# Two down projections in one stage, activations standing, with seven of sixteen tile pairs by Strassen's seven products

## The chip, the cores and the metric

The kernel runs on one core of a Trainium2 chip. The metric is device time in microseconds, the median of several runs of the whole kernel; lower is better.

## The reference

One transformer block over 256 tokens of width 2048 in float32: a modulated norm, input projections, a two-way recurrent mixer and a windowed attention, a gated merge, and a convolutional feed-forward part. The change lies in the last product of the feed-forward part:

```python
def conv_ffn(h, w_up, conv_w, conv_b, w_down):
    a, u = jnp.split(h @ w_up, 2, axis=-1)
    return (jax.nn.silu(depthwise_conv(a, conv_w, conv_b)) * u) @ w_down
...
        ffn_x = conv_ffn(modulate(x_mid, norm2_g[l], mod_x[:, 3], mod_x[:, 4]), w_up[l], conv_w[l], conv_b[l], w_down[l])
        new_x = x_mid + mod_x[:, 5][:, None, :] * ffn_x
```

The hidden width `D_FF` is 5632, so `w_down` is 5632 x 2048: 44 row tiles of 128 (called k or f) by 16 column tiles of 128 (called j).

## The kernel before

**Precision.** Every large product is split: an operand x becomes `hi`, a copy of x rounded to the fast float32 matmul type, and `lo` = x - `hi`. A product is then hi·hi + hi·lo + lo·hi, with float32 sums in PSUM. Activations are stored with hi and lo side by side (`gt[:, k, 1, :]` is hi, `gt[:, k, 0, :]` is lo, 256 tokens each).

**Weights.** They arrive as "halves" of 128 x 1024 values (512 KB), in the order in which they are used, in one array `wst`. `Stream.load` (line 107) takes one: a load on SyncE's queue into `raw` (4 buffers, L111), a copy on ScalarE into `whi` (3 buffers, L112), a subtraction on VectorE into `wlo` (3 buffers, L113). These three instructions carry a priority that is `LEAD` = 60 instructions earlier than where they are written, so they are placed ahead of the products that use them.

**Order.** The program is written out unrolled, and a planner orders each engine's instructions: among those that it takes to be ready, the one with the earliest priority goes first. Each engine then runs its list in that order; semaphores hold an instruction until its inputs and its buffer are there.

**Feed-forward stages.** The 44 hidden tiles are worked in groups of 16, 16 and 12 (`FF_GROUPS`): up 0, up 1, down 0, up 2, down 1, down 2. An up stage makes two columns of `w_up` a step by `duo` and evacuates them by `up_evac` (convolution, silu, product, split into `gt`). A down stage makes two output column tiles a step, also by `duo`, and adds each into the residual `xm` with the gate (`add`, L913: two `scalar_tensor_tensor` instructions of 128 x 256).

**`duo`.** Weights stand in the array, activations move. For each k and each of two output tiles, one 512-column matmul (weight hi against the activation's lo and hi) and one 256-column matmul (weight lo against the activation's hi). The output has output columns on partitions and tokens along the free side, as `xm` has.

**`natural`.** An earlier stage (line 451) uses the other form: activations stand, 512 columns of weights move, each product by `mm3` (three 512-column matmuls), and the output has tokens on partitions.

**Other names.** `ada` steps accumulate a modulation matrix on VectorE between other work (loads on GpSimd's queue, L378; sums, L383; transposes on TensorE, L391) and end in the gates; `gate2` is the last. PSUM has 8 banks: pool `mm` with 5, pool `ms` with 3. The SBUF slots "kT" and "va" hold the evacuation buffers `fs1` and `fs2` in the up stages; slot "v" holds `xa`, which is last read in the first columns of up 0.

Of the kernel before, what the change touches and what calls it, by code (L numbers as in the profile page):

```python
# [7 lines left out]
F32 = mybir.dt.float32  # L8
F32R = mybir.dt.float32r
U32 = mybir.dt.uint32  # L10
AF = mybir.ActivationFunctionType
ALU = mybir.AluOpType
AX = mybir.AxisListType

P = 128
T = 256
# [4 lines left out]
NFF = DFF // P  # L21
# [4 lines left out]
LEAD = 60  # L26
LAG = 60
RUSH = 120
# [4 lines left out]
CONSTS = [("ident", 128), ("ones", 128), ("ropec", 256), ("ropes", 256), ("amask", 256), ("hmask", 256),  # L33
          ("m64", T)]
FF_GROUPS = [(0, 16), (16, 16), (32, 12)]


def offsets(fields):
# [12 lines left out]
def block_kernel(ctx, tc, xct, prm, cst, ada2, wst, out):  # L51
    nc = tc.nc
    V, S, PE = nc.vector, nc.scalar, nc.tensor

    cons = ctx.enter_context(tc.tile_pool(name="cons", bufs=1))
    big = ctx.enter_context(tc.tile_pool(name="big", bufs=1))
    strm = ctx.enter_context(tc.tile_pool(name="strm", bufs=3))
    scr = ctx.enter_context(tc.tile_pool(name="scr", bufs=3))
    tiny = ctx.enter_context(tc.tile_pool(name="tiny", bufs=8))
    mm = ctx.enter_context(tc.tile_pool(name="mm", bufs=5, space=bass.MemoryType.PSUM))  # L60
    ms = ctx.enter_context(tc.tile_pool(name="ms", bufs=3, space=bass.MemoryType.PSUM))

    def bank(pool=None):
        pool = pool or mm
        return pool.tile([P, 512], F32, name="bank" + ("m" if pool is mm else "s"))

    def mmul(o, l, r, start, stop):
        return PE.matmul(o, l, r, start=start, stop=stop, skip_group_check=True)  # L68

    def mm3(o, lh, ll, rh, rl, start, stop):  # L70
        mmul(o, lh, rh, start, False)
        mmul(o, lh, rl, False, False)
        return mmul(o, ll, rh, False, stop)
# [11 lines left out]
    base = [1 << 30]  # L85
# [6 lines left out]
    def con(n):  # L92
        o, w = COFF[n]
        return cst_t[:, o:o + w]

    ident, ones = con("ident"), con("ones")
# [3 lines left out]
    class Stream:  # L100
# [26 lines left out]
        def next(self, n=1):  # L127
            if self.pos == 8:
                self.load()
            sl = slice(self.pos * P, (self.pos + n) * P)  # L130
            self.pos += n
            return self.hi[:, sl], self.lo[:, sl]

    st = Stream()

    def split(hi, lo, src):
        S.copy(hi, src)
        V.tensor_tensor(lo, src, hi.bitcast(F32), op=ALU.subtract)
# [41 lines left out]
    start = big.tile([P, 1024], F32, name="csr", tag="acc")  # L180
# [14 lines left out]
    def ada_mm(aps, u):  # L195
        n, per = len(chunks[u]), 4 // len(chunks[u])
        w = 256 * n
        for kt in range(KT):
            g, slot = 32 * (kt % 4), slots[groups[u][kt // 8 if n == 2 else 0] % 3][kt // per % 4]
            last_mm = mmul(aps[g:g + 32, 0:w], csr[:, kt, :], slot[:, kt % per * w:(kt % per + 1) * w], kt < 4, kt >= KT - 4)  # L200
        return last_mm
# [17 lines left out]
    def warm(n, after):  # L219
        with tc.issue_after(after.ins):  # L220
            for _ in range(n):
                last = mmul(ssq[:, 0:P], ident, ident, True, True)
        return last
# [35 lines left out]
    with tc.high_priority(offset=RUSH):  # L259
        for cnd in range(2):  # L260
            ts = slice(T * cnd, T * cnd + T)
# [4 lines left out]
    first = ada_mm(aps, 0)  # L266
    with tc.high_priority(offset=RUSH):
        first = warm(3, first)
# [9 lines left out]
    def unit(u):  # L278
        if len(chunks[u]) == 1:
            st.load(7)  # L280
            wv, w = [st.next(4)], [st.next() for _ in range(3)]
        else:
            st.load()
            wv = [st.next(4) for _ in range(2)]
            st.load(6)
            w = [st.next() for _ in range(6)]
        st.pos = 8
        return wv, w
# [19 lines left out]
    for u in range(len(chunks)):  # L308
        wv, w = unit(u)
# [91 lines left out]
    ada_it = ada_steps()  # L401

    def ada(n=1):
        with tc.high_priority(offset=-LAG), tc.issue_after(st.last.ins):
            for _ in range(n):
                next(ada_it, None)
# [3 lines left out]
    def tick():  # L410
        if tasks:
            tasks.pop(0)()

    def both(act, k):
        return act[:, k].rearrange("p a t -> p (a t)")
# [3 lines left out]
    def duo(acts, nk=KT):  # L419
        os = [bank() for _ in range(2)]  # L420
        for k in range(nk):
            ws = [st.next() for _ in range(2)]
            for o, w, act in zip(os, ws, acts):
                mmul(o, w[0], both(act, k), k == 0, k == nk - 1)
            for o, w, act in zip(os, ws, acts):
                mmul(o[:, T:], w[1], act[:, k, 1, :], False, k == nk - 1)
            if k % 4 == 3:
                tick()
        return os
# [160 lines left out]
    def hgrn_c(h):  # L590
        hs = slice(h * P, h * P + P)
        sp = bank(ms).rearrange("p (n d e) -> p n d e", n=2, d=2)
        for d in range(2):
            for a in range(2):
                PE.matmul(sp[:, 0, d], KN[:, d, a], vn[:, 2 + a, hs], start=(a == 0), stop=(a == 1))  # L595
            PE.matmul(sp[:, 1, d], KN[:, d, 2], vn[:, d, hs], start=True, stop=True)  # L596
        V.tensor_copy(SS[:, 0], sp[:, 0])
        for d in range(2):
            V.scalar_tensor_tensor(SS[:, 1, d], SS[:, 0, d], decb[:, d:d + 1], sp[:, 1, d], op0=ALU.mult, op1=ALU.add)

    def hgrn_d(h):
        hs = slice(h * P, h * P + P)
        ob = bank(ms)
        obs[h] = ob

        for a in range(2):
            mmul(ob[:, a * P:a * P + P], vn[:, a, hs], MS[:, a, :], a == 0, False)
        for d in range(2):
            for a in range(2):
                mmul(ob[:, a * P:a * P + P], SS[:, a ^ d, d], QI[:, d, a * P:a * P + P], False, d == 1)  # L610
        S.activation(OS[:, 0], ob[:, 0:T], AF.Square)

    def hgrn_e(h):
        if h < 0:
            return
        ob = obs.pop(h)
        PE.matmul(ob[:, T:], ones, OS[:, 0], start=True, stop=True)  # L617
        rsqrt(OS[:, 1], ob[:, T:], 1.0 / P)
        V.scalar_tensor_tensor(qo[:, 1, h, :], ob[:, 0:T], par("hng"), OS[:, 1], op0=ALU.mult, op1=ALU.mult)
# [50 lines left out]
    for h in range(H):  # L670
# [6 lines left out]
        if h == 6:  # L677
# [4 lines left out]
            kT = big.tile([P, 2, 512], F32, name="kT", tag="kT")  # L682
            va = big.tile([P, 4, 256], F32, name="va", tag="va")
            kv_evac(bs)
        for d in range(2):
            if 2 * h + d < 3:
                o = early_f[2 * h + d]
            else:
                o = bank()
# [4 lines left out]
        parts = [lambda h=h: hgrn_e(h - 1), lambda h=h: hgrn_b(h), lambda h=h: hgrn_c(h), lambda h=h: hgrn_d(h)]  # L694
        if h == 0:

            parts = [lambda: None, parts[1], lambda: None, parts[2], lambda: None, parts[3]]
# [126 lines left out]
    xm = big.tile([P, KT, T], F32, name="xm", tag="qo")  # L824
    for i in range(2):
        nc.sync.dma_start(xm[:, 8 * i:8 * i + 8, :], xct[:, 8 * i:8 * i + 8, 0:T])
    gate1, sc2, sh2, gate2 = [modv[:, i, :] for i in range(4)]
# [4 lines left out]
    g0 = hlf[:, 2 * KT * T:].rearrange("p (k a t) -> p k a t", a=2, k=KT)  # L832
# [53 lines left out]
    fs1 = big.tile([P, 4, T], F32, name="fs1", tag="kT")  # L886
    fs2 = big.tile([P, 4, T], F32, name="fs2", tag="va")
# [3 lines left out]
    def up_evac(g, gt, i, oa, ou, fold=fold):  # L891
        f = FF_GROUPS[g][0] + i
        t, s = fs1[:, f % 4, :], fs2[:, f % 4, :]
        fold(s, oa)
        S.activation(t, s, AF.Identity, bias=cb[:, f:f + 1], scale=cw[:, f, 1:2])  # L895
        V.scalar_tensor_tensor(t[:, 1:T], s[:, 0:T - 1], cw[:, f, 0:1], t[:, 1:T], op0=ALU.mult, op1=ALU.add)  # L896
        V.scalar_tensor_tensor(t[:, 0:T - 1], s[:, 1:T], cw[:, f, 2:3], t[:, 0:T - 1], op0=ALU.mult, op1=ALU.add)
        fold(s, ou)
        S.activation(t, t, AF.Silu)
        V.tensor_tensor(s, s, t, op=ALU.mult)  # L900
        split(gt[:, i, 1, :], gt[:, i, 0, :], s)
        if f >= 2:
            ada(1 + f % 2)

    def up(g, gt, i0=0):
        for i in range(i0, FF_GROUPS[g][1]):
            up_evac(g, gt, i, *duo((h2, h2)))

    def down(g, gt, last):
        f0, n = FF_GROUPS[g]  # L910
        def add(j, o):
            for i in range(2):
                V.scalar_tensor_tensor(xm[:, j, :], o[:, T * i:T * i + T], gate2[:, j:j + 1], xm[:, j, :],  # L913
                                       op0=ALU.mult, op1=ALU.add)

        for j in range(0, KT, 2):
            if last and j == KT - 2:
                for i in range(2):
                    add(j + i, single(gt, n))
                    nc.sync.dma_start(out[:, j + i:j + i + 1, :], xm[:, j + i:j + i + 1, :])  # L920
                continue
            for i, o in enumerate(duo((gt, gt), n)):
                add(j + i, o)
            j0 = {2: 0, 6: 4, 10: 8, 12: 12}.get(j)
            if last and j0 is not None:
                nc.sync.dma_start(out[:, j0:j + 2, :], xm[:, j0:j + 2, :])
# [3 lines left out]
    up(0, g0, 2)  # L930
    g1 = big.tile([P, 16, 2, T], F32R, name="g1", tag="b")
    up(1, g1)
    down(0, g0, False)
    up(2, g0)
    down(1, g1, False)
    down(2, g0, True)


# [154 lines left out]
```

## Time and profile before

| what | value |
|---|---|
| median of 3 runs | 1680.49 us (1680.35 to 1680.75) |
| profiled execution, first to last instruction (span) | 1680.0 us |
| TensorE (PE) busy | 1665.3 us (99%) |
| TensorE weight loads (PEld) busy | 1410.7 us (84%) |
| VectorE (DVE) busy | 1206.9 us (72%) |
| ScalarE (ACT) busy | 835.3 us (50%) |
| granted TensorE clock | 1.000 |

The page gives no time for the profiled execution other than its span; the median of the runs is 0.5 us above it. Busy is the time in which at least one instruction of an engine runs. PE and PEld are matmuls and weight loads, which overlap. In rows that list groups, `out<-in` names the tiles written and read, then follow the shape, the count, the busy time with the mean duration in ns, and the idle time before these instructions with what ended it. Rows of the chain or the timeline begin with the start and the length in us.

### The profile page before, as it was taken

The page shows a single profiled execution, that of the slowest core. Times are in us where ns is not written, and L with a number is a line of the kernel's source. Part 1 is how long each engine was busy: PE and PEld are TensorE (multiplying, and loading weights), DVE is VectorE, ACT ScalarE, POOL GpSimd, SP SyncE. Part 2 cuts the span into 40 slices and gives each one's busy share as a digit, 9 for nine tenths or more (in the row PEclk, how much of TensorE's full clock was granted, in tenths as well). Part 3 has the DMA queues.
Part 4 walks back from the last instruction along what each step waited for, and adds up shares of the span by engine and source line. Part 5 has one row for each costly group of instructions (what it writes and reads, how often), then busy time and mean ns, then how long its engine had stood idle before and what let it go on. Part 6 is the DMA issues. An engine that isn't in the chain of part 4 may idle for free.

```text
span 1680.0 us, 25442 instructions
## 1 busy us (share of the span) xinstructions
PE 1665.3 (99%) x9774; PEld 1410.7 (84%) x9774; DVE 1206.9 (72%) x1920; ACT 835.3 (50%) x1279; POOL 68.3 (4%) x132
## 2 busy tenths in 40 slices
PE   7999999999999999999999999999999999999999
PEld 4668888888888888888888988888888888888887
DVE  3448986666879886879879887777666656666565
ACT  4337543433646764455555655555555335554332
POOL 0000100000000000001000000000000000000000
PEclk9999999999999999999999999999999999999999
DMA  9987834534466668878866577687555555555564
GB/s 380 407 350 242 288 119 160 177 110 155 162 217 208 211 209 278 285 243 279 282 199 234 185 251 250 218 272 251 188 182 194 188 188 189 188 188 189 188 201 150
DMA packets 104154, 371.88 MB, mean 221 GB/s; under 512 B 11488, under 2 KB 13920, under 8 KB 104032
## 3 DMA queue, kind: packets, MB, share of 16 engines
q1 hardware_dynamic: 85600, 303.14, 52.8%
q0 software_dynamic: 18432, 67.12, 12.7%
q8 instruction: 76, 1.25, 0.3%
q14 instruction: 46, 0.38, 0.1%
HBM read 368.11 MB, written 2.10 MB: 220 GB/s over the span
## 4 chain that ended last, share of the span: by engine, by line
PE 93%; DMA 4%; issue 2%; DVE 1%; SPq 0%; ACT 0%; POOL 0%; DVEq 0%; POOLq 0%
PE bankm L68 87%; PE banks L68 4%; DMA ringv<-in_wst_dram 1%; DMA ringq<-in_wst_dram 1%; DMA ringkT<-in_wst_dram 1%; DVE wlo L113 1%; PE banks L391 0%; PE banks L595 0%; PE banks L764 0%; DMA araw<-in_ada_dram 0%; PE banks L587 0%; DMA xraw<-in_xct_dram 0%; PE banks L596 0%; PE banks L617 0%; PE banks L734 0%
## 5 line engine op out<-in xcount | busy, mean ns | idle before, releaser
L68 PE MATMUL bankm<-hl,whi 128*128 128x512 f32 (+1 forms) x3392 | 1050.6, 392 | 0.0
L113 DVE TENSOR_TENSOR wlo<-raw,whi 128x1024 fp32r<-128x1024 f32 (+1 forms) x498 | 606.7, 1219 | 314.1 <-ACT whi L112 312.3
L112 ACT CAST whi<-raw 128x1024 fp32r<-128x1024 f32 (+1 forms) x498 | 520.9, 1046 | 588.4 <-PE bankm L68 499.4
L68 PEld LDWEIGHTS bankm<-hl,wlo 128*128 128x128 f32 x3104 | 581.4, 188 | 133.7 <-DVE wlo L113 2.1
L68 PE MATMUL bankm<-hl,wlo 128*128 128x256 f32 (+2 forms) x3104 | 660.5, 287 | 1.2 <-DVE wlo L113 1.2
L68 PEld LDWEIGHTS bankm<-hl,whi 128*128 128x128 f32 x3392 | 533.8, 189 | 19.9 <-DVE fs L882 0.3
L68 PE MATMUL bankm<-whi,hl 128*128 128x512 f32 x512 | 164.7, 395 | 1.0 <-ACT hl L230 1.0
L383 DVE SCALAR_TENSOR_TENSOR acc<-araw,csil,acc 128x1024 f32<-128x1024 f32 x120 | 153.5, 1279 | 2.2 <-DMA araw<-in_ada_dram 1.8
L68 PEld LDWEIGHTS bankm<-whi,hl 128*128 128x128 f32 x512 | 95.7, 188 | 22.3 <-ACT hl L230 2.6
L378 POOL DMA_DIRECT2D araw<-in_ada_dram x128 | 68.1, 532 | 1093.5 <-DVE acc L383 579.2
L68 PE MATMUL bankm<-wlo,hl 128*128 128x512 f32 x256 | 99.6, 392 | 0.0
L68 PE MATMUL bankm<-yb,whi 128*128 128x512 f32 x256 | 80.8, 397 | 0.0
L68 PE MATMUL bankm<-g,whi 128*128 128x512 f32 x256 | 80.4, 395 | 0.0
L68 PEld LDWEIGHTS bankm<-g,wlo 128*128 128x128 f32 x256 | 48.1, 188 | 11.4
L68 PEld LDWEIGHTS bankm<-yb,wlo 128*128 128x128 f32 x256 | 48.1, 188 | 11.3
L68 PEld LDWEIGHTS bankm<-wlo,hl 128*128 128x128 f32 x256 | 48.0, 188 | 9.8 <-DVE wlo L113 0.2
L913 DVE SCALAR_TENSOR_TENSOR xm<-bankm,modv,xm 128x256 f32<-128x256 f32 x96 | 42.2, 480 | 18.3 <-PE bankm L68 18.3
L895 ACT ACTIVATE fs<-fs,prm 128x256 f32<-128x256 f32 x44 | 26.5, 602 | 56.2 <-DVE fs L449 56.2
L68 PE MATMUL bankm<-yb,wlo 128*128 128x256 f32 x256 | 50.6, 279 | 0.0
L68 PE MATMUL bankm<-g,wlo 128*128 128x256 f32 x256 | 50.3, 278 | 0.0
L896 DVE SCALAR_TENSOR_TENSOR fs<-fs,prm,fs 128x255 f32<-128x255 f32 x44 | 21.3, 484 | 26.7 <-ACT fs L895 26.7
L211 DVE TENSOR_REDUCE tn<-banks 128x8 f32<-128x32 f32 (+1 forms) x9 | 1.7, 188 | 53.3 <-ACT whi L112 50.4
(218 smaller groups left out, 1203.7 us busy)
## 6 DMA issues: line engine op xcount, KB each, us to landing
raw<-in_wst_dram SPq DMA_DIRECT2D x489, 512.0 KB, 4.2
araw<-in_ada_dram POOLq DMA_DIRECT2D x128, 512.0 KB, 4.8
ringv<-in_wst_dram SPq DMA_DIRECT2D x24, 512.0 KB, 10.0
ringq<-in_wst_dram SPq DMA_DIRECT2D x20, 512.0 KB, 9.9
araw<-in_wst_dram SPq DMA_DIRECT2D x10, 512.0 KB, 9.9
xraw<-in_xct_dram SPq DMA_DIRECT2D x8, 512.0 KB, 6.7
raw<-in_wst_dram SPq DMA_DIRECT2D x7, 384.0 KB, 9.9
ringkT<-in_wst_dram SPq DMA_DIRECT2D x5, 512.0 KB, 9.9
```

The source lines that it names most:

```text
L68: return PE.matmul(o, l, r, start=start, stop=stop, skip_group_check=True)
L112: S.copy(hi, raw)
L113: self.last = V.tensor_tensor(lo, raw, hi.bitcast(F32), op=ALU.subtract)
L211: V.tensor_reduce(m8, aps[:, 0:w].rearrange("p (q g c) -> p q c g", q=2 * n, g=4)[:, :, 0:2, :], axis=AX.X, op=ALU.add)
L378: nc.gpsimd.dma_start(raw, ada2[idx])
L383: V.scalar_tensor_tensor(acc, raw, csil[:, kt, 0:1], acc, op0=ALU.mult, op1=ALU.add)
L895: S.activation(t, s, AF.Identity, bias=cb[:, f:f + 1], scale=cw[:, f, 1:2])
L896: V.scalar_tensor_tensor(t[:, 1:T], s[:, 0:T - 1], cw[:, f, 0:1], t[:, 1:T], op0=ALU.mult, op1=ALU.add)
L913: V.scalar_tensor_tensor(xm[:, j, :], o[:, T * i:T * i + T], gate2[:, j:j + 1], xm[:, j, :], op0=ALU.mult, op1=ALU.add)
```

## The change

The first two down groups (32 of the 44 row tiles) become one stage, `down_two`, which runs after up 1 and before up 2; the third stays as it was. In `down_two` the activations stand and the weights move, 512 columns a matmul. The stage works the output in two halves of 1024 columns (`half`), each 16 pairs of row tiles long. A pair is a 2 x 2 block product: token tiles 1 and 2, row tiles k1 and k2, column blocks of 512.

Nine pairs (`p` not in `SEVEN`) make all eight block products into four PSUM banks `norm`. Seven pairs make seven products by Strassen's method (in Winograd's form): three sums of activations (made once in the up stage by `seven_acts` and kept), four sums of weights t1 to t4 (made on VectorE for each pair and half: `two` and `four`), and products that go into `norm` and into four further banks `sev`. The sum chunks pass through tile `araw` (2 buffers) and are split into `whi` and `wlo` like loaded ones. After the last seven-pair `sev` is combined into SBUF tiles `y`; after the last pair `norm` is added to them. `turn` transposes `y` on TensorE (16 transposes a half) and adds it to `xm` with the gate. The first half's `turn` is written after pair 0 of the second half and uses the banks that become that half's `sev`.

For the first row tile of a seven-pair `up_evac` splits only the first 128 tokens; the place of the other 128 holds the difference of the two token tiles, split by `seven_acts`. The `ada` steps left over, if any, are run before `down_two`. The weight array is laid out anew for the stage (64 halves as before). The store for descriptors of GpSimd's loads is set to 8192 bytes a partition.

```diff
+SEVEN = (1, 3, 5, 7, 9, 11, 13)
...
+    def chunk(parts, make, tag="raw"):
+        with tc.high_priority(offset=min(LEAD, max(0, tc.tile_snap_priority() - base[0]))):
+            raw = strm.tile([P, 1024], F32, name=tag, bufs=4 if tag == "raw" else 2)
+            hi, lo = [strm.tile([P, 1024], F32R, name=nm, bufs=3) for nm in ("whi", "wlo")]
+            make(raw)
+            w = slice(0, 512 * parts)
+            S.copy(hi[:, w], raw[:, w])
+            V.tensor_tensor(lo[:, w], raw[:, w], hi[:, w].bitcast(F32), op=ALU.subtract)
+        return raw, [(hi[:, 512 * i:512 * i + 512], lo[:, 512 * i:512 * i + 512]) for i in range(parts)]
+
+    def fetch(raw):
+        nc.sync.dma_start(raw, wst[st.half])
+        st.half += 1
...
-        split(gt[:, i, 1, :], gt[:, i, 0, :], s)
+        if g < 2 and f // 2 in SEVEN:
+            if f % 2:
+                split(gt[:, i, 1, :], gt[:, i, 0, :], s)
+                seven_acts(f // 2, gt, i, fs2[:, (f - 1) % 4, :], s)
+            else:
+                split(gt[:, i, 1, 0:P], gt[:, i, 0, 0:P], s[:, 0:P])
+        else:
+            split(gt[:, i, 1, :], gt[:, i, 0, :], s)
...
+    def seven_acts(p, gt, i, s1, s2):
+        if not sums:
+            sums["a"] = big.tile([P, 5, 2, 3 * P], F32R, name="sa", tag="v")
+            sums["b"] = big.tile([P, 2, 2, 3 * P], F32R, name="sb", tag="sb")
+        n = SEVEN.index(p)
+        d = sums["a"][:, n] if n < 5 else sums["b"][:, n - 5]
+        sums[p] = d
+        w = scr.tile([P, 512], F32, name="t")
+        V.tensor_tensor(w[:, 0:P], s1[:, P:], s2[:, P:], op=ALU.subtract)
+        V.tensor_tensor(s1[:, P:], s1[:, P:], s1[:, 0:P], op=ALU.subtract)
+        V.tensor_tensor(w[:, P:2 * P], s1[:, 0:P], w[:, 0:P], op=ALU.subtract)
+        V.tensor_tensor(w[:, 2 * P:3 * P], s2[:, 0:P], w[:, P:2 * P], op=ALU.subtract)
+        split(gt[:, i - 1, 1, P:], gt[:, i - 1, 0, P:], s1[:, P:])
+        split(d[:, 0, :], d[:, 1, :], w[:, 0:3 * P])
...
+    def half(n, g0, g1, norm, sev, y, before):
...
+        def add(b, a, w, start=False, stop=False):
+            mm3(b, *a, *w, start, stop)
+        first = SEVEN[0]
+        for p in range(16):
+            k1, k2 = 2 * p, 2 * p + 1
+            rb, (w21, w22) = chunk(2, fetch)
+            a11, a21, a12, a22 = act(k1, 0), act(k1, 1), act(k2, 0), act(k2, 1)
+            if p not in SEVEN:
...
+                add(norm[0], a12, w21, st0)
+                add(norm[2], a22, w21, st0)
+                add(norm[1], a12, w22, st0)
+                add(norm[3], a22, w22, st0)
+                ra, (w11, w12) = chunk(2, fetch)
+                add(norm[0], a11, w11)
+                add(norm[2], a21, w11)
+                add(norm[1], a11, w12)
+                add(norm[3], a21, w12)
+                if p == 0:
+                    before()
+                continue
+            f, l = p == first, p == SEVEN[-1]
+            d = sums[p]
+            s1, s2, s4 = [(d[:, 0, i * P:i * P + P], d[:, 1, i * P:i * P + P]) for i in range(3)]
+            add(norm[0], a12, w21)
+            add(norm[1], s4, w22)
+            ra, (w11,) = chunk(1, fetch)
+            add(sev[0], a11, w11, f, l)
+
+            def two(raw):
+                V.tensor_tensor(raw[:, 0:512], ra[:, 0:512], ra[:, 512:], op=ALU.add)
+                V.tensor_tensor(raw[:, 512:], ra[:, 512:], rb[:, 512:], op=ALU.add)
+            r2, (t1, t3) = chunk(2, two, "araw")
+            add(sev[1], s1, t1, f, l)
+            add(sev[3], a21, t3, f, l)
+
+            def four(raw):
+                V.tensor_tensor(raw[:, 0:512], r2[:, 0:512], rb[:, 512:], op=ALU.add)
+                V.tensor_tensor(raw[:, 512:], raw[:, 0:512], rb[:, 0:512], op=ALU.add)
+            r4, (t2, t4) = chunk(2, four, "araw")
+            add(sev[2], s2, t2, f, l)
+            add(norm[2], a22, t4)
+            if l:
+                y12, y34 = y
+                S.copy(y12[:, 0], sev[0])
+                V.tensor_tensor(y34[:, 0], sev[2], y12[:, 0], op=ALU.subtract)
+                V.tensor_tensor(y12[:, 1], sev[1], y34[:, 0], op=ALU.add)
+                V.tensor_tensor(y34[:, 0], sev[3], y34[:, 0], op=ALU.add)
+                V.tensor_tensor(y34[:, 1], sev[3], y12[:, 1], op=ALU.add)
+        with tc.high_priority(offset=RUSH):
+            for b in range(4):
+                o = y[b // 2][:, b % 2]
+                V.tensor_tensor(o, norm[b], o, op=ALU.subtract if b == 2 else ALU.add)
+
+    def turn(n, y, banks):
+        for q in range(4):
+            o = banks[q] if banks else bank(ms)
+            for i in range(2):
+                for tt in range(2):
+                    c = (2 * q + i) * P
+                    src = y[tt][:, c // 512, c % 512:c % 512 + P]
+                    PE.transpose(o[:, i * T + tt * P:i * T + tt * P + P], src, ident)
+            for i in range(2):
+                j = 8 * n + 2 * q + i
+                V.scalar_tensor_tensor(xm[:, j, :], o[:, i * T:i * T + T], gate2[:, j:j + 1], xm[:, j, :],
+                                       op0=ALU.mult, op1=ALU.add)
+
+    def down_two(g0, g1):
+        ys = lambda: [big.tile([P, 2, 512], F32, name="y" + t, tag=t) for t in ("kT", "va")]
+        sev = [bank()]
+        norm = [bank() for _ in range(4)]
+        sev += [bank(ms) for _ in range(3)]
+        y0 = ys()
+        half(0, g0, g1, norm, sev, y0, lambda: None)
+        norm = [bank()] + [bank(ms) for _ in range(3)]
+        sev = [bank() for _ in range(4)]
+        y1 = []
+        half(1, g0, g1, norm, sev, y1, lambda: (turn(0, y0, sev), y1.extend(ys())))
+        turn(1, y1, None)
...
-    down(0, g0, False)
+    for _ in ada_it:
+        pass
+    down_two(g0, g1)
+    fs1 = big.tile([P, 4, T], F32, name="fs1", tag="kT")
+    fs2 = big.tile([P, 4, T], F32, name="fs2", tag="va")
     up(2, g0)
-    down(1, g1, False)
     down(2, g0, True)
...
+    nc = bacc.Bacc("TRN2", target_bir_lowering=False, num_devices=1, dynamic_dma_scratch_size=8192)
```

More of the change, by code (lines that the diff above doesn't have):

```diff
@@ L900, in up_evac @@
         V.tensor_tensor(s, s, t, op=ALU.mult)
-        split(gt[:, i, 1, :], gt[:, i, 0, :], s)
+        if g < 2 and f // 2 in SEVEN:
[6 more added lines that the diff above has]
+            split(gt[:, i, 1, :], gt[:, i, 0, :], s)
         if f >= 2:
             ada(1 + f % 2)
+    sums = {}
+    def seven_acts(p, gt, i, s1, s2):
[12 more added lines that the diff above has]
+        split(d[:, 0, :], d[:, 1, :], w[:, 0:3 * P])
     def up(g, gt, i0=0):
@@ L907, in up, with act @@
             up_evac(g, gt, i, *duo((h2, h2)))
+    def half(n, g0, g1, norm, sev, y, before):
+        def act(k, tt):
+            gt = g0 if k < 16 else g1
+            ts = slice(tt * P, tt * P + P)
+            return gt[:, k % 16, 1, ts], gt[:, k % 16, 0, ts]
+        def add(b, a, w, start=False, stop=False):
[6 more added lines that the diff above has]
+            if p not in SEVEN:
+                st0, sp = p == 0, p == 15
+                if sp:
+                    ra, (w11, w12) = chunk(2, fetch)
+                    for b, u1, u2, v1, v2 in ((0, a11, a12, w11, w21), (1, a11, a12, w12, w22), (2, a21, a22, w11, w21),
+                                              (3, a21, a22, w12, w22)):
+                        add(norm[b], u1, v1)
+                        add(norm[b], u2, v2, stop=True)
+                    break
+                add(norm[0], a12, w21, st0)
+                add(norm[2], a22, w21, st0)
+                add(norm[1], a12, w22, st0)
+                add(norm[3], a22, w22, st0)
+                ra, (w11, w12) = chunk(2, fetch)
+                add(norm[0], a11, w11)
[35 more added lines that the diff above has]
+                V.tensor_tensor(o, norm[b], o, op=ALU.subtract if b == 2 else ALU.add)
@@ L1073, in downs @@
         d = dnt[:, f0:f0 + n]
-        if i < 2:
-            return _duos(np, d)
         return np.concatenate([_duos(np, d[:KT - 2]), _halves(np, d[KT - 2:])], 0)
-    parts += [ups(0), ups(1), downs(0), ups(2), downs(1), downs(2)]
+    pairs = g["w_down"][0].reshape(NFF // 2, 2, P, 2, 1024)[:16, ::-1].transpose(3, 0, 1, 2, 4).reshape(-1, P, 1024)
+    parts += [ups(0), ups(1), pairs, ups(2), downs(2)]
     wst = np.concatenate(parts, 0)
     arrays = {"xct": xct, "prm": prm, "cst": _constants(np), "ada2": ada2, "wst": wst}
-    nc = bacc.Bacc("TRN2", target_bir_lowering=False, num_devices=1)
+    nc = bacc.Bacc("TRN2", target_bir_lowering=False, num_devices=1, dynamic_dma_scratch_size=8192)
     feed, args = {}, []
```

## The prediction

> **What bounds the kernel now.** I read the page's busy shares and its chain first, then the chain in order of time, then the groups by shape.
>
> ```profile
> span 1680.0 us, 25442 instructions
> PE 1665.3 (99%) x9774; PEld 1410.7 (84%) x9774; DVE 1206.9 (72%) x1920; ACT 835.3 (50%) x1279; POOL 68.3 (4%) x132
> PE 93%; DMA 4%; issue 2%; DVE 1%; SPq 0%; ACT 0%; POOL 0%; DVEq 0%; POOLq 0%
> ...
> 252.31 5.46 PE bankm L68 x24
> 257.77 0.43 PE banks L617 x2
> ...
> 1218.91 0.22 PE banks L391 x2
> 1219.13 81.05 PE bankm L68 x465
> ...
> 1219.13 457.01 PE bankm L68 x2624
> ```
>
> TensorE is 99% busy, but the page warns that a busy PE is not PE at its peak: matmul durations overlap. Cost must be read as pitch (start to start). From 1219 us to 1676 us the chain is one unbroken run of 2624 matmuls, 457.01 / 2624 = 0.1742 us each. It holds the end of the second up group, down 0, the third up group, down 1 and down 2. So TensorE alone sets the time where the change lies, and only fewer TensorE microseconds, or a new wait of TensorE, can move it.
>
> ```profile
> L68 PE MATMUL bankm<-hl,whi 128*128 128x512 f32 x3264 | 1027.2, 396 | 0.0
> L68 PE MATMUL bankm<-hl,wlo 128*128 128x256 f32 x2816 | 555.0, 279 | 1.2 <-DVE wlo L113 1.2
> ...
> 252.62 0.62 PE L68 MATMUL bankm<-whi,hl 128*128 128x512 f32 x2
> 253.07 0.39 PE L68 MATMUL bankm<-wlo,hl 128*128 128x512 f32 x1
> 253.30 0.62 PE L68 MATMUL bankm<-whi,hl 128*128 128x512 f32 x2
> ```
>
> Today one 128x128 weight tile is a 512-column matmul and a 256-column matmul, weights standing. The durations 396 and 279 would make 0.675 us; the chain says 2 x 0.1742 = 0.348 us. The form that the change uses, activations standing and 512 columns of weights moving, exists already in `natural`: the group at 252.31 us, 24 matmuls in 5.46 us, 0.2275 us each with the next chain piece starting exactly when it ends; the timeline shows three of them from 252.62 to 253.30, again 0.227 each.
>
> **The change part by part.**
>
> *TensorE, form.* The two downs have 32 x 16 weight tiles: 1024 matmuls at 0.1742 = 178.3 us. All products in the new form: per pair and column half, 2 k tiles x 2 token tiles x 2 column blocks = 8 products of 3 matmuls; 16 pairs x 2 halves x 24 = 768 at 0.2275 = 174.7 us. Gain 3.6 us: the same 393,216 columns in a quarter fewer instructions.
>
> [...]
>
> *TensorE, seven products.* Seven pairs x 2 halves lose one product of three matmuls: 42 x 0.2275 = 9.55 us. 726 matmuls remain, 165.2 us.
>
> *TensorE, transposes.* The output comes out token-major, so `turn` adds 32 transposes of 128x128. The L391 transposes have a pitch of 0.11 us (two in 0.22): 3.6 us, all on the path, since TensorE has no free time. TensorE sum: 165.2 + 3.6 = 168.8 against 178.3, a gain of 9.5 us. Nothing else can give more.
>
> *VectorE and ScalarE, weights.* Every 1024 columns of weights are copied (L112) and subtracted (L113). A seven-pair splits 3.5 such chunks instead of 2 and adds four 512-wide sums.
>
> ```profile
> L113 DVE TENSOR_TENSOR wlo<-raw,whi 128x1024 fp32r<-128x1024 f32 x489 | 597.8, 1223 | 311.7 <-ACT whi L112 310.0 <-issue 0.3
> L112 ACT CAST whi<-raw 128x1024 fp32r<-128x1024 f32 x489 | 513.3, 1050 | 585.8 <-PE bankm L68 499.4 <-issue 73.9 <-ACT hl L137 6.1
> L913 DVE SCALAR_TENSOR_TENSOR xm<-bankm,modv,xm 128x256 f32<-128x256 f32 x96 | 42.2, 480 | 18.3 <-PE bankm L68 18.3
> L138 DVE TENSOR_TENSOR ab<-banks,ab 128x512 fp32r<-128x512 f32 x20 | 13.0, 683 | 0.8 <-ACT ab L137 0.8
> L539 DVE TENSOR_TENSOR hb<-hb 128x512 f32<-128x512 f32 x16 | 11.0, 689 | 0.2
> ...
> 1297.30:1386.40 89.10, 89.10 (x513) 77.74 (x512) 52.69 (x67) 35.41 (x38) 0.00 (x0) 1.00 0.59 189
> 757.70:879.00 121.30, 121.30 (x699) 105.85 (x698) 100.75 (x145) 61.81 (x97) 8.44 (x16) 1.00 0.78 257
> ```
>
> In the last two rows the columns are TensorE, weight load, VectorE, ScalarE, GpSimd, clock, DMA share. VectorE in a seven-pair: 3 x 1.223 + 0.688 (the half chunk) + 4 x 0.689 = 7.11 us, beside 21 x 0.2275 = 4.78 us of TensorE. In a plain pair: 2 x 1.223 = 2.45 beside 24 x 0.2275 = 5.46. Seven-pairs and plain pairs alternate, so two pairs hold 9.56 us of VectorE and 10.24 of TensorE. ScalarE: (3.5 + 2) x 1.05 = 5.8, no bound. VectorE goes from 59% of the stage (52.69 / 89.10, down 0) to 93% between the edges. Now 757.70 to 879.00 shows 100.75 / 121.30 = 83% VectorE with TensorE fully busy; 93% no row shows. That is the change's unpriced point. From below: no wait at all, 0. From above: VectorE in strict program order, waiting out each ScalarE copy of a sum before subtracting it, 9.56 + 2 x (1.05 + 0.03) = 11.72 us in two pairs against 10.24, so 14 x 1.48 = 20.7 us.
>
> ```profile
> 1249.60 1.05 ACT L112 CAST whi<-raw 128x1024 fp32r<-128x1024 f32 x1 [1.43 <-PE bankm L68]
> 1250.68 1.23 DVE L113 TENSOR_TENSOR wlo<-raw,whi 128x1024 fp32r<-128x1024 f32 x1 [1.23 <-ACT whi L112]
> ...
> 241.08 0.42 DVE L583 TENSOR_TENSOR hb<-hb 128x256 f32<-128x256 f32 x1
> 241.41 0.43 DVE L518 TENSOR_SCALAR hb<-hb 128x512 f32<-128x512 f32 x1
> 241.75 1.22 DVE L113 TENSOR_TENSOR wlo<-raw,whi 128x1024 fp32r<-128x1024 f32 x1
> 242.88 0.69 DVE L523 TENSOR_TENSOR_SCAN hb<-cst,hb 128x256 f32<-128x256 f32 x1
> ...
> ACT whi L112 <- PE bankm L68: 50.0, 29, 1.8
> DVE wlo L113 <- ACT whi L112: 28.2, 21, 1.6
> SPq L111 <- DVE wlo L113: 66.6, 28, 2.6
> raw<-in_wst_dram SPq DMA_DIRECT2D x28, 512.0 KB, 4.0
> ```
>
> These rows are hand-over times (ACT ends 1250.65, VectorE starts 1250.68), VectorE's own pitch (each starts about 0.08 before its forerunner ends) and, last four, waits and loads in down 0. What ends ScalarE's wait is TensorE: a copy waits for one of three hi buffers, so the splits run as far ahead as the buffers let them. I walked a seven-pair with three buffers, from the start of its first product. r2 (first two sums) takes the buffer that the plain pair frees at 0: copied by 1.08, subtracted by 2.33. TensorE wants its hi at 3 x 0.6825 = 2.05 and its lo one matmul later, 2.28: about 0.05 late. r4 takes the buffer of the first chunk, free after two products plus the matmul's drain, about 1.6: copied by 2.65, subtracted by 3.9; wanted at 5 x 0.6825 = 3.41 and 3.64: about 0.25 late. The sums themselves need no hi buffer and fit into VectorE's wait for r2's copy and the plain pair before. The next plain pair's chunk is subtracted by 5.1, in time for 4.78 + 0.23. So the walk gives 0.2 to 0.3 us a seven-pair, and I take 0.2, since VectorE's overlap (0.08 a step, eight steps) works against it: 14 x 0.2 = 2.8 us. I take a value near the lower end because 83% already runs at no cost, nearer to 93% than strict order is to anything in the trace.
>
> *Loads.* 64 loads of 512 KB before and after, in 169 instead of 178 us. A raw buffer comes round every 10.24 us (four buffers, four loads in two pairs), and landing takes 4.0; a seven-pair's is held until the fourth sum, so up to 6 us of hold is free. Price 0; the waits of SP's queue for L113 (66.6 us in 28) say it is ahead today.
>
> *Edges.* At entry two of the eight banks belong to the last up column and come free after its evacuation; the other two norm banks have two products each on both chunks (2.7 us) for cover. At the turn between halves VectorE adds 8 evacuations of about 0.69 and 8 `scalar_tensor_tensor` of 0.48 (9.4 us) over three plain pairs whose slack is 3 x 3.0 = 9.0. At the exit the last bank's evacuation (0.69) stands before the last transposes, and the third up group can fill in. L913's 64 steps fall away (64 x 0.48 = 31 us of VectorE), against the turns' 16 x 0.48. I take 0.7 us for the three edges, from 0 to 6 (each bare: 0.69 + 0.4 at the exit, some 2.5 at the other two).
>
> *Up stages.* The activation sums (`seven_acts`) add per pair four 128-wide steps, a 384-wide and a 128-wide subtraction, less a shortened one.
>
> ```profile
> 1130.00:1216.00 86.00, 86.00 (x496) 75.03 (x496) 63.93 (x86) 46.79 (x71) 2.64 (x5) 1.00 0.66 221
> L538 DVE TENSOR_TENSOR hb<-hb 128x128 f32<-128x128 f32 x32 | 8.1, 285 | 0.0
> L138 DVE TENSOR_TENSOR g<-fs,g 128x256 fp32r<-128x256 f32 x16 | 6.7, 419 | 0.0
> ```
>
> With 0.285 at 128 and about 0.55 at 384 (between 0.419 and 0.683) that is 1.84 us of VectorE in a pair's 64 x 0.348 = 22.3 us, raising 74% to 82%, less than the 83% seen above with TensorE full. Price 0; were VectorE late there, 14 pairs x 0.3 would be 4 us. The ada steps left for the drain loop are none: their last transposes (L391) end at 1219.13, inside the second up group. The smaller descriptor store concerns only GpSimd's 128 loads, all done by then; price 0, and as no load of this stage uses it, no loss beyond that stretch.
>
> *Sum.* 168.8 + 2.8 + 0.7 = 172.3 against 178.3: 6.0 us less. The span 1680.0 becomes 1674.0; the median of the runs, 1680.49, stands 0.5 above the span, so 1674.5.
>
> **The rivals.**
>
> *Slower: VectorE's order becomes the bound.* If subtractions of sums stand directly behind their copies, every pair of pairs takes 11.72 us: 168.8 + 20.7 + 0.7 = 190.2, 12 us more, 1692. It decides from the point where two pairs cost VectorE 10.24 + 9.5 / 14 = 10.9 us elapsed. For it: in down 0, 21 of 28 subtractions already stand behind their copy, 28.2 us in all, where that costs nothing. Against it: VectorE has other chunks' sums and splits to put there, and the 83% stretch. So a fifth, not a half. [...]
>
> *No change: the gain is eaten.* Lateness of 0.39 to 0.87 us a seven-pair (5.4 to 12.2 us in all) gives 174.9 to 181.7 us: 1677.1 to 1683.9, centre 1680.5. For it: the r4 buffer is late in my walk already, and any queueing on VectorE adds to it. [...]
>
> *Raw buffers run dry.* If seven-pairs held theirs over 6 us, loads would set the pace; with 8 us of hold each two pairs cost 2 us more: 168.8 + 0.7 + 28 = 197.5, 1700. Landing at 4.0 us speaks against it.
>
> **How the numbers follow.** A measurement of this kernel tells about 0.2%, 3.4 us, from no change. Forecast (lateness under 0.39 us a seven-pair): 0.61, 1671 to 1677. Eaten: 0.18, of which 0.02 for the form. VectorE's order: 0.18. Raw buffers: 0.03. The floor is 1680.5 - 9.5 = 1671; I put the low end at 1670.5. At the high end half of the slower cases, those under half of the strict-order price, are taken in: 1687. Faster 0.61, same 0.18, slower 0.18 + 0.03 = 0.21.
>
> **What would show it.** Matmuls of the stage at 0.2275 pitch, 726 of them, and 32 transposes near 0.11: the stage near 172 us. TensorE waiting for `wlo` or `whi` a few tenths at a time, after the fifth product of a seven-pair, if the walk is right; for over 0.5 us there, or ScalarE's copies behind sums, if the rival is. VectorE near 90% of the stage. The up stages at an unchanged 0.1742. I am wrong if TensorE's waits in the stage pass 6 us, or if 0.2275 does not hold with eight banks in turn.

## The result, and the profile after

| kernel | median | runs | ratio to before (95% interval) |
|---|---|---|---|
| before | 1680.75 us (1680.29 to 1681.99) | 7 | |
| changed | 1675.49 us (1675.09 to 1676.99) | 7 | 0.9969 (0.9958 to 0.9980) |

The change makes the kernel 5.3 us faster, 0.3%; 6.0 were forecast. The page of the changed kernel, first the busy shares, then its chain of work:

```profile
span 1673.8 us, 25069 instructions
PE 1660.3 (99%) x9508; PEld 1392.2 (83%) x9508; DVE 1264.6 (76%) x2014; ACT 862.1 (52%) x1323; POOL 68.3 (4%) x132
...
PE 96%; DMA 2%; DVE 1%; ACT 0%; issue 0%; SPq 0%; DVEq 0%; ACTq 0%
```

TensorE has 266 instructions fewer (298 matmuls of products less, 32 transposes more) and still fills 99% of a shorter span; VectorE rose from 72% to 76%.

The spans differ by 6.2 us, but 1.1 us of that lies before the stage: the first matmul of the first down came at 1297.00 us before and at 1295.89 after, although nothing ahead of up 0 was changed (in the two chains one and the same piece, 23.21 us of matmuls, begins at 627.79 before and at 626.66 after), and the kernels below begin the stage anywhere from 1295.8 to 1297.5. So I compare kernels by the time from the stage's first matmul to the start of the last twelve matmuls of the kernel. The timeline rows for it, the first two of before, the last two of after:

```profile
1297.00 0.62 PE L68 MATMUL bankm<-hl,whi 128*128 128x512 f32 x2
1674.54 1.59 PE L68 MATMUL bankm<-hl,wlo 128*128 128x256 f32 x12
```

```profile
1295.89 0.40 PE L69 MATMUL bankm<-whi,hl 128*128 128x512 f32 x1
1668.39 1.59 PE L69 MATMUL bankm<-hl,wlo 128*128 128x256 f32 x12
```

377.54 before, 372.50 after: 5.0 us less. The new stage itself is 5.8 us shorter (172.5 against 178.3 for the two down groups), and 0.8 come back behind it, where the last four transposes stand among the third up group's matmuls. Now the chain of the changed kernel in order of time, in the steady part of the first half:

```profile
1306.41 7.71 PE bankm L69 x34
1314.12 1.83 PE banks L69 x7
1315.95 0.23 PE bankm L69
1316.18 0.47 PE banks L69 x2
1316.64 7.96 PE bankm L69 x35
...
1327.12 7.99 PE bankm L69 x35
```

One seven-pair and one plain pair, 45 matmuls, take 1327.12 - 1316.64 = 10.48 us. At 0.2275 they would take 10.24. Something holds TensorE a quarter of a microsecond in each. The waits of the whole stage name it, and the timeline of one seven-pair shows where (PEld rows are weight loads):

```profile
ACT whi L143 <- PE bankm L69: 36.6, 36, 3.7
...
PEld bankm L69 <- DVE wlo L144: 2.6, 7, 0.4
PEld banks L69 <- DVE wlo L144: 2.6, 7, 0.4
...
PEld bankm L69 <- ACT whi L143: 0.9, 2, 0.7
```

```profile
1321.89 0.69 DVE L999 TENSOR_TENSOR araw<-araw,raw 128x512 f32<-128x512 f32 x1
...
1322.40 0.39 PE L69 MATMUL bankm<-whi,hl 128*128 128x512 f32 x1
1322.64 1.05 ACT L143 CAST whi<-araw 128x1024 fp32r<-128x1024 f32 x1 [2.14 <-DVE araw L999]
...
1323.73 2.59 DVE L144 TENSOR_TENSOR wlo<-araw,whi 128x1024 fp32r<-128x1024 f32 x2 [1.15 <-ACT whi L143]
...
1324.44 0.39 PE L69 MATMUL banks<-whi,sa 128*128 128x512 f32 x1
1324.44 0.19 PEld L69 LDWEIGHTS banks<-whi,hl 128*128 128x128 f32 x1
1324.67 0.39 PE L69 MATMUL banks<-whi,hl 128*128 128x512 f32 x1
...
1325.01 0.19 PEld L69 LDWEIGHTS banks<-wlo,sa 128*128 128x128 f32 x1 [0.38 <-DVE wlo L144]
1325.01 0.50 PE L69 MATMUL banks<-wlo,sa 128*128 128x512 f32 x1
...
1325.35 0.40 PE L69 MATMUL banks<-whi,sa 128*128 128x512 f32 x1
```

The wait for `wlo` comes 14 times. Thirteen times it is the weight load of a matmul on the `wlo` of r2, once in each seven-pair but the first of the second half. The fourteenth (1383.39, in plain pair 0 of the second half) and the two waits for ScalarE's copies (1390.51 and 1391.45, in the first seven-pair of that half) lie at the turn between the halves. The seven-pair shown starts at 1322.40. Ahead of that matmul went the plain pair's last; r2's copy starts 0.24 later, the first of the two subtractions ends near 1324.95 (1323.73 + 1.22). The planner had already put both hi matmuls of r2 first; the lo matmul was due at 1324.67 + 0.2275 = 1324.90. It starts at 1325.01, and the starts around it are 0.34 apart instead of 0.23: being some 0.06 late costs 0.23, because the wait stands at the weight load (188 ns), which otherwise starts with the matmul ahead and hides under it (1324.44 and 1324.67 above). The row puts the copy's wait down to the sum L999, which ended just then (1321.89 + 0.69); in the stage's totals such waits are mostly TensorE's, 36 of them. Which of the two it is, two experiments had to tell.

VectorE in the stage and in the up stage (columns as before: TensorE, weight load, VectorE, ScalarE):

```profile
1295.89:1468.40 172.51, 172.28 (x756) 136.54 (x755) 149.56 (x177) 92.73 (x100) 0.00 (x0) 1.00 0.59 195
1130.00:1216.00 86.00, 86.00 (x496) 75.04 (x495) 66.38 (x99) 48.07 (x74) 2.64 (x5) 1.00 0.63 217
```

149.56 / 172.51 = 87%, against 59% in down 0 before, with TensorE all but full.

### The profile page after: what moved, and what is told of

Its sections match the earlier page's. It is cut to its first block, busy times and chain, and to the rows that moved or that the text cites. A ratio compares the mean times of both kernels' runs of the same rounds, so it can differ in the third digit from the quotient of the medians.

```text
span 1673.8 us, 25069 instructions
## 1 busy us (share of the span) xinstructions
PE 1660.3 (99%) x9508; PEld 1392.2 (83%) x9508; DVE 1264.6 (76%) x2014; ACT 862.1 (52%) x1323; POOL 68.3 (4%) x132
## 4 chain that ended last, share of the span: by engine, by line
PE 96%; DMA 2%; DVE 1%; ACT 0%; issue 0%; SPq 0%; DVEq 0%; ACTq 0%
PE bankm L69 85%; PE banks L69 9%; DMA ringv<-in_wst_dram 1%; DMA ringq<-in_wst_dram 1%; PE banks L406 0%; PE banks L610 0%; PE banks L779 0%; PE banks L602 0%; DVE wlo L114 0%; DMA xraw<-in_xct_dram 0%; PE banks L611 0%; PE banks L224 0%; PE banks L632 0%; PE banks L749 0%; PE banks L1022 0%
## 5 line engine op out<-in xcount | busy, mean ns | idle before, releaser
L69 PE MATMUL bankm<-hl,whi 128*128 128x512 f32 (+1 forms) x3136 | 970.4, 392 | 0.0
L114 DVE TENSOR_TENSOR wlo<-raw,whi 128x1024 fp32r<-128x1024 f32 (+2 forms) x434 | 528.1, 1218 | 240.0 <-ACT whi L113 238.2
L113 ACT CAST whi<-raw 128x1024 fp32r<-128x1024 f32 (+2 forms) x434 | 453.2, 1045 | 479.5 <-PE bankm L69 366.4
L69 PEld LDWEIGHTS bankm<-hl,wlo 128*128 128x128 f32 x2848 | 533.2, 188 | 120.6 <-DVE wlo L114 0.4
L69 PE MATMUL bankm<-hl,wlo 128*128 128x256 f32 (+2 forms) x2848 | 610.2, 287 | 0.0
L69 PEld LDWEIGHTS bankm<-hl,whi 128*128 128x128 f32 x3136 | 494.9, 189 | 20.3 <-DVE hl L153 0.4
L69 PE MATMUL bankm<-whi,hl 128*128 128x512 f32 x640 | 209.2, 395 | 1.2 <-ACT hl L245 1.0
L143 ACT CAST whi<-raw 128x1024 fp32r<-128x1024 f32 x64 | 61.1, 956 | 42.1 <-PE bankm L69 25.4
L144 DVE TENSOR_TENSOR wlo<-raw,whi 128x1024 fp32r<-128x1024 f32 x64 | 69.3, 1104 | 2.2 <-ACT whi L143 1.1
L69 PE MATMUL bankm<-whi,g 128*128 128x512 f32 x136 | 46.1, 390 | 0.0
```

Source lines behind the costliest of these rows:

```text
L113: S.copy(hi, raw)
L114: self.last = V.tensor_tensor(lo, raw, hi.bitcast(F32), op=ALU.subtract)
L143: S.copy(hi[:, w], raw[:, w])
L144: V.tensor_tensor(lo[:, w], raw[:, w], hi[:, w].bitcast(F32), op=ALU.subtract)
```

## The experiments

Theory: the seven products gain 9.55 us, the new form pays for the transposes, and what is lost is one stall a seven-pair, made by three `whi` buffers. Rivals: VectorE's load makes the stall; or the form brings the gain and the sums eat what Strassen saves. "Stage" below is the time from the stage's first matmul to the last twelve, as above: before 377.5, changed 372.5. The experiments ran in two further sessions, in which the kernel before took 1680.62 us (the first two below, no weight sums and strict order) and 1681.71 us (the others), and each ratio is to the kernel before of its own session; differences between kernels are therefore best read from the stage.

### No seven-pairs

```diff
-SEVEN = (1, 3, 5, 7, 9, 11, 13)
+SEVEN = ()
...
-                V.tensor_tensor(o, norm[b], o, op=ALU.subtract if b == 2 else ALU.add)
+                V.tensor_copy(o, norm[b])
```

> No seven-pairs: all 16 pairs of a half make eight products, no sums, y is a plain copy of the four norm banks; transposes as in the changed kernel. Theory (the form gives 3.6 us, the transposes take 3.6 back, and the seven products give 9.55 us less one stall of 0.22 us a seven-pair, 6.4 net): 768 x 0.2275 + 3.6 + about 1 at the edges = 179.3 us for the stage, 1681 to 1682, that is no better than the kernel before. Rival (the form gives all, the sums on VectorE eat what Strassen saves): 1675 to 1676, as the changed kernel.

Measured: 1680.24 us, ratio 0.9999 (0.9990 to 1.0007); stage 377.4. That is 0.8 us below the range that I gave: the pitch is a little shorter and the edges cost almost nothing. The form gives just what the transposes take, and the rival that gave it the whole gain falls. All of the 5 us is Strassen's.

### A fourth whi buffer

```diff
-            hi, lo = [strm.tile([P, 1024], F32R, name=nm, bufs=3) for nm in ("whi", "wlo")]
+            hi, lo = [strm.tile([P, 1024], F32R, name=nm, bufs=b) for nm, b in (("whi", 4), ("wlo", 3))]
...
-... dynamic_dma_scratch_size=8192)
+... dynamic_dma_scratch_size=7168)
```

(the last two lines are cut short; and the same count in `Stream.load`, which shares the buffers)

> One edit: four whi buffers instead of three (and a descriptor store of 7168 bytes to make room). Theory (each seven-pair's one stall of 0.22 us comes from r2's copy waiting for the whi buffer that the plain pair's last matmul frees, then 1.05 + 1.22 us of copy and subtraction): r2 can be copied earlier, the 14 stalls go, 3.1 us less: 1672 to 1673. Rival (VectorE's load of 87% makes r2 late): no change, 1675 to 1676.

Measured: 1671.91 us, ratio 0.9948 (0.9936 to 0.9961), 0.1 us below the range that I gave; stage 367.7, 4.8 less than the changed kernel. Its chain in order of time:

```profile
1306.97 8.16 PE bankm L69 x36
1315.13 2.04 PE banks L69 x9
1317.17 8.16 PE bankm L69 x36
1325.33 2.04 PE banks L69 x9
1327.37 8.16 PE bankm L69 x36
```

Its busy times in the stage:

```profile
1297.01:1464.40 167.39, 167.39 (x751) 138.44 (x750) 147.71 (x175) 91.88 (x100) 0.00 (x0) 1.00 0.59 201
```

45 matmuls in 10.20 us, none waiting; TensorE is busy through all 167.39 us, with VectorE at 88%. So the floor of a pair of pairs is 10.20 (0.2267 a matmul). In the changed kernel it is 10.50 from one stall to the next (1325.01 to 1335.51): 0.23 at the wait, and 0.07 in the matmuls behind it, whose starts are up to 0.01 further apart. The thirteen stalls make 3.7 of the 4.8 us (0.30 each, the first 0.2). Another 0.9 went at the turn between the halves (from the start of pair 14 to the start of the next half's pair 2: 23.77 us there, 22.90 here), and 0.3 behind the stage's last product. The fastest kernel of the study.

### A fourth wlo buffer instead

```diff
-            hi, lo = [strm.tile([P, 1024], F32R, name=nm, bufs=3) for nm in ("whi", "wlo")]
+            hi, lo = [strm.tile([P, 1024], F32R, name=nm, bufs=b) for nm, b in (("whi", 3), ("wlo", 4))]
```

(again with the same count in `Stream.load`, and with the descriptor store of 7168 bytes)

> Four wlo buffers and three whi buffers: the same room as the run with four whi buffers, given to the other tile. Theory (r2's copy waits for a whi buffer; its wlo buffer is free before the subtraction anyway): no change, 1675 to 1677. Rival (any fourth buffer, or the other placing in memory, takes the stalls away): 1671.5 to 1672.5.

Measured: 1676.11 us, ratio 0.9966 (0.9953 to 0.9978); stage 372.5, as the changed kernel to the hundredth. It is the `whi` buffer, not the room or the other tile.

### No weight sums

```diff
             def two(raw):
-                V.tensor_tensor(raw[:, 0:512], ra[:, 0:512], ra[:, 512:], op=ALU.add)
-                V.tensor_tensor(raw[:, 512:], ra[:, 512:], rb[:, 512:], op=ALU.add)
-            r2, (t1, t3) = chunk(2, two, "araw")
+                pass
+            r2, (t1, t3) = chunk(2, two, ra)
...
```

(and r4 likewise from rb; `chunk` then takes the tile that it is given in place of a new one; without the sums the output is not the reference's)

> The four weight sums of each seven-pair are left out: r2 and r4 are split from the loaded ra and rb, so the products are made with wrong weights at the same cost; VectorE loses 4 x 0.69 us a seven-pair, 38 us in the stage (87% to about 65%). Theory (a whi buffer, not VectorE, sets r2's time): the stalls stay, 1675 to 1676. Rival (VectorE's load): the stalls go, 1672 to 1673.

Measured: 1676.28 us, ratio 0.9974 (0.9964 to 0.9984), 0.3 us above the range; stage 371.8. Its busy times in the changed kernel's stretch (its own stage begins 0.4 us later):

```profile
1295.89:1468.40 172.51, 172.30 (x759) 137.70 (x758) 117.30 (x122) 92.86 (x100) 0.00 (x0) 1.00 0.58 195
```

Its wait for r2, in one pair of pairs (1314 to 1324.5 us):

```profile
PEld banks L69 <- DVE wlo L144: 0.3, 1, 0.3
```

VectorE fell from 149.56 to 117.30 us and the stall is still in the same thirteen seven-pairs. Leaving out four sums a pair gains 0.7 us in the whole stage; the rival of VectorE's load falls, and so does L999 as the releaser.

### VectorE in strict order

```diff
+                with tc.issue_after(st.sub.ins):
-                V.tensor_tensor(raw[:, 0:512], r2[:, 0:512], rb[:, 512:], op=ALU.add)
-                V.tensor_tensor(raw[:, 512:], raw[:, 0:512], rb[:, 0:512], op=ALU.add)
+                    V.tensor_tensor(raw[:, 0:512], r2[:, 0:512], rb[:, 512:], op=ALU.add)
+                    V.tensor_tensor(raw[:, 512:], raw[:, 0:512], rb[:, 0:512], op=ALU.add)
```

(`st.sub` is the last subtraction made by `chunk`, here that of r2; only these two sums are tied, the rest is ordered as planned)

> VectorE's two sums of a four are ordered behind the subtraction of r2 (same work, strict program order). The prediction's slow rival in the flesh. If its price holds as bounded (1.48 us in each two pairs against 10.24): about 1693. If TensorE can fill the wait for r4 with ready products of the next plain pair and the buffers hold: r4 is copied by 5.0 instead of 2.65 us after the pair's start, wanted at 3.4, so between 0.3 and 1.6 us a seven-pair, 1679 to 1697. Under 1677 would say that the order of the sums does not matter.

Measured: 1712.16 us, ratio 1.0191 (1.0175 to 1.0207), 37 us more than the changed kernel and beyond both ends that I gave; stage 406.0, 33.5 more. The timeline around one r4:

```profile
1314.26 1.05 ACT L143 CAST whi<-araw 128x1024 fp32r<-128x1024 f32 x1 [2.14 <-PE bankm L69]
...
1315.34 1.23 DVE L144 TENSOR_TENSOR wlo<-araw,whi 128x1024 fp32r<-128x1024 f32 x1 [2.35 <-ACT whi L143]
...
1316.48 0.69 DVE L999 TENSOR_TENSOR araw<-araw,raw 128x512 f32<-128x512 f32 x1
...
1317.20 0.69 DVE L1000 TENSOR_TENSOR araw<-araw,raw 128x512 f32<-128x512 f32 x1
...
1318.01 1.04 ACT L143 CAST whi<-araw 128x1024 fp32r<-128x1024 f32 x1 [2.70 <-DVE araw L1000]
...
1319.10 0.50 PE L69 MATMUL banks<-whi,sa 128*128 128x512 f32 x1 [1.28 <-ACT whi L143]
```

The waits of its stage:

```profile
ACT whi L143 <- DVE araw L1000: 35.0, 14, 3.1
```

The chain is the one of the prediction, but it starts anew in each seven-pair, at the buffer that TensorE frees: VectorE stands idle 2.35 us ahead of r2's subtraction, and the two sums come only behind it (1316.48 and 1317.20). TensorE gets no filler either, since the next plain pair's copy stands behind r4's on ScalarE, which is idle 2.70 us ahead of r4's. The gaps before r4's first matmul add about 1.45 us in twelve of the 14 seven-pairs, with some 0.6 more behind them; where the clock stays full, two pairs take 12.53 us (from 1316.62 to 1329.15).

### Eight seven-pairs, with four and with three whi buffers

```diff
-SEVEN = (1, 3, 5, 7, 9, 11, 13)
+SEVEN = (1, 3, 5, 7, 8, 10, 12, 14)
...
-            sums["b"] = big.tile([P, 2, 2, 3 * P], F32R, name="sb", tag="sb")
+            sums["b"] = big.tile([P, 3, 2, 3 * P], F32R, name="sb", tag="sb")
```

(with a descriptor store of 4096 bytes, and once with the four `whi` buffers of above)

> Four whi buffers and eight seven-pairs, 1, 3, 5, 7, 8, 10, 12, 14 (7 and 8 side by side; descriptor store 4096 bytes for the further sums). TensorE's floor falls by 2 x 0.6825 = 1.4 us: 1670.5 against 1671.9 if VectorE keeps up. VectorE in pairs 7 to 9 has 2 x 7.11 + 2.45 = 16.7 us beside 15.0 of TensorE; if that shows, 1 to 1.7 us a half come back: 1672.5 to 1674.

> Eight seven-pairs as above with three whi buffers. TensorE's floor falls by 1.4 us, two more stalls of 0.22 us come: 1674.5 if that were all. In pair 8 the half chunk's subtraction would end some 7.2 us after pair 7's start by VectorE's durations, wanted at 6.15, and the sums of r4 follow: 1 to 2.5 us late a half, 1676 to 1680.

Measured: four buffers 1673.49 us, ratio 0.9953 (0.9941 to 0.9966), stage 369.3; three buffers 1680.40, ratio 0.9992 (0.9983 to 1.0001), stage 376.3, in time 0.4 us above the range that I gave. Either way the eighth pair, placed so, costs more than the 1.4 us that it saves: the stage is 1.6 us longer than in the four-buffer kernel with seven, and 3.8 longer than in the changed kernel. With four buffers TensorE stops once in each half for 0.85 us in the second of the two adjacent seven-pairs; the rest of the loss lies at the turn and near the ends of the halves (the new list also moves the last seven-pair from 13 to 14). With three, the waits between 1337 and 1344 us of that kernel:

```profile
PEld banks L69 <- ACT whi L143: 2.1, 2, 1.1
...
PEld banks L69 <- DVE wlo L144: 0.2, 1, 0.2
```

Two further stops near 0.9 us a half, now for copies, and a rougher turn.

### Transposes twice

```diff
+                    for _ in range(2):
-                    PE.transpose(o[:, i * T + tt * P:i * T + tt * P + P], src, ident)
+                        PE.transpose(o[:, i * T + tt * P:i * T + tt * P + P], src, ident)
```

> Each of the 32 transposes is done twice. Theory (they are on TensorE's path at 0.11 us each): 3.5 us more, 1678.5 to 1679.5. Rival (they lie in time that TensorE waits anyway at the turns): 1675 to 1676.

Measured: 1679.33 us, ratio 0.9987 (0.9978 to 0.9996); stage 376.3, 3.8 more. They are on the path: 3.5 of the 3.8 are the 32 transposes at 0.11, and the remaining 0.3 is what the other waits at the turn and at the end changed on balance.

## Why the prediction was right

**TensorE sum (9.5 us).** Right in each term. Form less transposes was 0.0: measured 0.2 (no seven-pairs). Seven products 9.55: measured 9.7 (stage 377.4 against 367.7, both without stalls). The whole, 9.8, against 9.5: the matmul pitch of the new form is 0.2267 here.

**The lateness (2.8 us).** The mechanism was right, a chunk waiting for a hi buffer, and so was which rule sets it; place and size were off. The walk let r2's copy start at 0, the end of the plain pair; for r4 I had counted the matmul's drain, for r2 not. The trace has 0.24 us there, so r2 and not r4 makes the stall. And I took lateness at its face: 0.06 us late costs 0.23 at once and 0.30 in all, because the weight load comes out from under its cover. Term: 3.7 (thirteen stalls) instead of 14 x 0.2 = 2.8. r4 arrives in time, since the planner puts its two hi matmuls ahead. That the size came out so near is luck: I charged the chunk that is in time, and let go the one that the walk itself had 0.05 late.

**Edges (0.7).** Measured 1.1: 0.9 at the turn, where copies and subtractions come late, 0.3 behind the last product, and about 0.1 less at the entry, each against the kernel with four `whi` buffers.

**VectorE's load.** 87% was forecast as "near 90%" and harmless; without the sums the stage is only 0.7 us shorter. In the up stage I had 82%, measured 77% (66.38 / 86.00): only every other pair there is a seven-pair, which I forgot (for the same reason "14 pairs" there should be seven). The price of 0 stands: a chain piece of 824 matmuls of the up stage takes 143.53 us before and 143.52 after.

**Loads.** The price of 0 was right as well: the waits of the stage hold a single one for a load, 0.5 us, on VectorE.

**The upper bound.** This step failed. 20.7 us for strict order took VectorE's work and two copies as one running total (11.72 us for two pairs), so that time lost in one pair could be made up in the next. But VectorE is tied to TensorE's releases (in the rows above, r2's copy waits 2.14 us for TensorE and its subtraction 2.35 for the copy), and the two pairs took 12.53 us. Against the kernel without stalls, the like of that sum, the stage is 38.3 us longer (406.0 against 367.7); some 6.8 of it, by my estimate, is half clock (0.50 for 4 x 3.41 us), which is told below and which no term of the prediction had. The case was given a fifth and a range up to 1687; had the planner made that order, the range would have missed by 25 us.

**From span to time.** I set the median 0.5 us above the span. In the runs listed it is 1.8 (1675.49 for a span of 1673.7), so the profiled execution of before was probably some 1.3 us slower than its median. This shifts the absolute time alone, not the forecast difference.

**A small sum.** 32 transposes at 0.11 are 3.5 us, not 3.6; that does not move the forecast.

**Sum.** -9.8 (TensorE) + 3.7 (stalls) + 1.1 (edges) = -5.0, measured -5.0 in the stage and -5.3 in the medians. The forecast was -9.5 + 2.8 + 0.7 = -6.0: the gain was put 0.3 too low, the losses 1.3 too low.

## What to carry to other kernels

Where TensorE is full, count its instructions by pitch from the chain (here 0.2267 us a matmul), never by the durations of the rows (0.39), and then ask of each staged operand which buffer it waits for. In this stage an engine at 87% was harmless, while one buffer of 4 KB a partition was worth almost as much as the whole change (4.8 us of stage against 5.0). Let the walk begin at the release of the buffer, matmul drain and hand-over included (together 0.24 us here), and give the extra buffer to the tile whose release starts the chain. A bound on an engine in strict order must restart at each release; a running total understates it (here 11.72 us for two pairs, where 12.53 were measured).

## What the runs showed of the hardware that was not expected

In these traces a late operand cost more than its lateness. I take as lateness the end of the subtraction less the time at which the matmul was due (start of the one ahead plus 0.2267), and as cost what the two starts around the wait take beyond 2 x 0.2267. In thirteen seven-pairs without weight sums 0.02 us late cost 0.18 to 0.19; in twelve of the changed kernel 0.06 cost 0.22 to 0.23; with eight pairs and three buffers 0.23 (the load at 1403.31) cost 0.40, and 0.09 early (1377.71) still cost 0.08; with the transposes done twice 0.54 (1383.96) cost 0.70. So in these traces the cost is the lateness plus 0.16 to 0.17: the operand had to be there that long before its matmul was due, in time for the weight load (0.19 us).

In the strict-order kernel the clock dropped behind gaps of 1.29 us. Behind the one that ends at 1331.63 us, the matmuls' pitch doubled to 0.43 us for some 3.5 us (columns: TensorE, weight load, VectorE, ScalarE, GpSimd, clock):

```profile
1332.50:1336.10 3.60, 3.52 (x9) 2.76 (x10) 3.21 (x4) 1.69 (x3) 0.00 (x0) 0.54 0.40 131
1336.10:1345.00 8.90, 8.34 (x36) 6.32 (x34) 5.04 (x6) 2.38 (x4) 0.00 (x0) 0.99 0.41 142
```

The timeline of the same place, a matmul before and one in the slow stretch:

```profile
1331.63 0.50 PE L69 MATMUL banks<-whi,sa 128*128 128x512 f32 x1 [1.29 <-ACT whi L143]
...
1333.44 0.63 PE L69 MATMUL banks<-wlo,sa 128*128 128x512 f32 x1
```

It followed four of the 14 gaps, in which TensorE is idle for 0.8 to 1.5 us each, mostly 1.3 and 0.2 more shortly behind. The granted clock in the four stretches:

```profile
1332.80:1336.22 3.42, 3.42 (x9) 2.66 (x9) 2.91 (x4) 1.50 (x2) 0.00 (x0) 0.50 0.37 116
1360.11:1363.52 3.41, 3.41 (x10) 2.63 (x9) 3.25 (x4) 1.04 (x1) 0.00 (x0) 0.50 0.51 169
1373.76:1377.18 3.42, 3.42 (x10) 2.68 (x9) 2.83 (x4) 1.52 (x2) 0.00 (x0) 0.50 0.43 135
1424.96:1428.38 3.42, 3.42 (x9) 2.67 (x8) 2.94 (x4) 1.39 (x2) 0.00 (x0) 0.50 0.45 160
```

Each lasts 3.41 us with TensorE busy throughout, so I estimate that they cost half of 4 x 3.41, some 6.8 us. The mean clock of the whole execution, 0.996 over 1707.3 us, is that of four such stretches.

The gaps ahead of the four end at 1331.63, 1358.24, 1372.40 and 1423.46 us; in each TensorE is idle for 1.29 us, and for 0.22 more just behind. No half clock followed eight gaps of 1.26 to 1.29 us with the same 0.22 behind them, nor the longest, 1.47 us (it ends at 1306.58). So the length of the gap does not tell the four from the other ten, and this one trace does not show what does.
